# The weights of a one-core diffusion layer, laid out so that each partition's part of a buffer slot is one run in memory

## The chip, the cores and the metric

The kernel runs on one core of a Trainium2 chip. The metric is the device time of one execution in microseconds (us), lower is better. The core has a matrix engine (PE, with its weight loads shown apart as PEld), a vector engine (DVE), a scalar engine (ACT), GpSimd (POOL) and a sequencer for transfers (SP). SP issues every load of this kernel; 16 DMA engines carry them out in the order of issue. A transfer is carried as packets; a packet moves one run of bytes that is contiguous at both ends.

## The reference, cut to what matters

```python
mod = jax.nn.silu(c) @ w_ada[l] + b_ada[l]                 # w_ada 1024 x 6144: six vectors for scale, shift and gate
h = modulate(rms_norm(x, g_pre_mix[l]), sh1, sc1)          # x: 256 tokens x 1024
q, k, v, su, sv = split_projection(h @ w_in[l] + b_in[l])
...                                                        # windowed attention beside spatial gating (sgu_w)
mix = merge_heads(attn_o, sgu_o, ..., w_out[l], b_out[l])  # w_out 1024 x 1024
x_mid = x + gt1 * rms_norm(mix, g_post_mix[l])
h2 = modulate(rms_norm(x_mid, g_pre_ffn[l]), sh2, sc2)
# 32 experts, each token goes to its top 4 by h2 @ w_router + b_router; for an expert's tokens xb:
gu = xb @ w_gate_up[e] + b_gate_up[e]                      # w_gate_up[e]: 1024 x 2048
act = (up + 1) * gate * jax.nn.sigmoid(SWIGLU_ALPHA * gate)
y = act @ w_down[e] + b_down[e]                            # w_down[e]: 1024 x 1024
x_new = x_mid + gt2 * rms_norm(ffn, g_post_ffn[l])
```

All numbers are float32. The experts' weights are 32 x 12 MB, and all of them are read, whatever the routing.

## The kernel before

**Stages.** The first part (up to about 194 us) computes the mixing sub-layer and the routing. Its order is the text `PLAN`, a list of step names; a step is a Python generator (`step(...)`) whose pieces run as its name comes up. Then a loop goes over the 32 experts. For an expert, `gu_chunk` multiplies the expert's up to 64 tokens by four chunks of `w_gate_up` (64 matmuls into the PSUM banks `pg` and `pu`), `swiglu` and `to_ff` make the activations on DVE, ACT and PE, and `down` multiplies them by two chunks of `w_down` (32 matmuls into `py`). Experts come in pairs: `gather_pair` makes the pair's tokens (`gx`), `combine` adds the pair's results to the output (`cb`). An expert with more than 64 tokens takes the branches `more_gu` and `more_down` (bank `pm`); two of the 32 do with these inputs, and the branch is jumped over for the others.

**Slots.** Weights lie in ten slots of 128 partitions x 16 KB (2 MB each), made by `slot`; slot 6 is two halves of 8 KB per partition (`slot_halves`, tiles `we_a` and `we_b`). `order` gives the turn of the slots and `todo` the order of the loads: `load_chunk` for the chunks of an expert (four of `w_gate_up`, two of `w_down`), `load_gt2` for two pieces of `w_ada`, and `load_columns` at the end for `w_down` of the last two experts, by columns. `load_more(n)` issues the next n loads; SP waits in each until the slot's former content is used up. Loads for the experts begin during the first part (`ring` in `PLAN`).

**Where the bytes lie.** In memory the weights lie as in the reference, row by row. A slot of `w_gate_up` takes 256 rows of 8 KB: partition p gets rows p and 128 + p, two runs of 8 KB. A slot of `w_down` takes 512 rows of 4 KB: four runs of 4 KB a partition. `load_ada` takes 256 columns at a time out of rows of 24 KB (runs of 1 KB), and `load_columns` 512 or 256 columns (runs of 2 KB or 1 KB). In the halves of slot 6 the runs are as long as in a whole slot. All loads go through `load`, which is `SY.dma_start`; in profiles they have the line of the helper that records every operation (L114).

Of the kernel before, what the change touches and what calls it, by code (L numbers as in the profile page):

```python
# [20 lines left out]
P = 128  # L21
D = 1024
T = 256
KD = D // P
HEADS = 8
HD = 64
NE = 32
SL = 64
SM = 32
NSLOT = 10  # L30
# [52 lines left out]
def kernel(  # L83
# [5 lines left out]
    rows: bass.AP,  # L89
    cst: bass.AP,  # L90
    w_ada: bass.AP,
    w_in: bass.AP,
    w_out: bass.AP,
    sgu_w: bass.AP,
# [1 line left out]
    w_gate_up: bass.AP,  # L96
    b_gate_up: bass.AP,
    w_down: bass.AP,
    b_down: bass.AP,
    out: bass.AP,  # L100
):
# [28 lines left out]
    def slot(i, name, dt=F32):  # L130
        return ring.tile([P, 4096], dt, tag=f"s{i}", name=name)

    def slot_halves(i, name, dt=F32):

        if i == SPLIT:
            return [ring.tile([P, 2048], dt, tag=f"s{i}{h}", name=f"{name}_{h}") for h in "ab"]
        w = slot(i, name, dt)
        return [w[:, 0:2048], w[:, 2048:4096], w]
# [5 lines left out]
    def load(dst, src):  # L144
        SY.dma_start(out=dst, in_=src)
# [58 lines left out]
    ada = []  # L204
    win = [None] * KD

    def load_ada(i):
        a = slot(i % 2, f"ada{i}").rearrange("p (k c) -> p k c", k=KD)
        src = w_ada.rearrange("(k p) c -> p k c", p=P)
        load(a[:, :, 0:256], src[:, :, 256 * i:256 * i + 256])  # L210
        load(a[:, :, 256:512], src[:, :, D + 256 * i:D + 256 * i + 256])
        ada.append(a)

    def load_win(i):
        w = slot(2 + i % 2, f"win{i}")[:, 0:2 * 1792].rearrange("p (k c) -> p k c", k=2)
# [11 lines left out]
    hT, cT = s8[:, 0], s8[:, 1]  # L227
    kvs = slot(7, "kvs", FR).rearrange("p (k s c) -> p k s c", k=KD, s=2)
    load_ada(0)
    load_win(0)  # L230
    load_ada(1)


# [22 lines left out]
    wr = pre.tile([P, KD, NE], F32, name="wr")  # L256
    halves = [slice(0, 512), slice(512, 1024)]
# [9 lines left out]
    tiles = {}  # L267
# [215 lines left out]
    ada2 = {}  # L483

    def load_mod(i, j, a):
        a = a.rearrange("p (k c) -> p k c", k=4)
        load(a, w_ada[512 * j:512 * j + 512, D * i:D * i + D].rearrange("(k p) c -> p k c", p=P))
        return a

    def mod_half(pm, a, j):  # L490
        for b in range(4):
# [10 lines left out]
           adav[:, 8 * i:8 * i + 8].rearrange("p (n c) -> p n c", n=2), ADD)  # L502

    def load_rest(j, sl):
        a = slot(sl, f"adb{j}").rearrange("p (k c) -> p k c", k=2)
        load(a, w_ada[256 * j:256 * j + 256, 2048:4096].rearrange("(k p) c -> p k c", p=P))
        ada2[j] = a
        yield

    def load_scale2(j, sl):  # L510
        tiles["sc2", j] = load_mod(4, j, slot(sl, f"adc{j}"))
        yield

    def load_ws():
        wsraw = slot(0, "ws")[:, 0:1024].rearrange("p (h j) -> p h j", h=HEADS)
        load(wsraw, sgu_w.rearrange("h i j -> i h j"))
        tiles["ws"] = wsraw
        yield

    def load_wr():  # L520
        load(wr, w_router.rearrange("(k p) e -> p k e", p=P))
        yield

    def load_context():
# [8 lines left out]
    wo = [None, None]  # L533

    def load_wo(i, sl):
        w = slot(sl, f"wo{i}").rearrange("p (k c) -> p k c", k=4)
        load(w, w_out[512 * i:512 * i + 512, :].rearrange("(k p) c -> p k c", p=P))
        wo[i] = w
        yield


# [9 lines left out]
    order = [6, 9, 1, 3, 7, 4, 8, 0, 2, 5]  # L551
    cursor = [0]
    chunks = {}

    def load_weights(e, rows, srcs):

        halves = slot_halves(order[cursor[0] % NSLOT], f"we{e}_{cursor[0]}")
        cursor[0] += 1
        w = [h.rearrange("p (k c) -> p k c", k=rows // 2) for h in halves[0:2]]
        for c, src in srcs:  # L560
            src = src.rearrange("(k p) c -> p k c", p=P)
            if len(halves) > 2:
                load(halves[2].rearrange("p (k c) -> p k c", k=rows)[:, :, c], src)
            else:
                for i in range(2):
                    load(w[i][:, :, c], src[:, rows // 2 * i:rows // 2 * (i + 1), :])
        return w

    def load_chunk(e, j):

        if j < 4:
            return load_weights(e, 2, [(slice(0, 2048), w_gate_up[e, 256 * j:256 * j + 256, :])])
        return load_weights(e, 4, [(slice(0, D), w_down[e, 512 * (j - 4):512 * (j - 3), :])])

    def load_columns(e, n, step):

        return load_weights(e, 8, [(slice(c, c + step), w_down[e, :, 512 * n + c:512 * n + c + step])
                                   for c in range(0, 512, step)])

    gt2_parts = []  # L580

    def load_gt2(j):
        gt2_parts.append(load_mod(5, j, slot(order[cursor[0] % NSLOT], f"adg{j}")))
        cursor[0] += 1

    todo = [(load_chunk, (e, j)) for e in range(NE) for j in range(6 if e < NE - 2 else 4)]
    todo += [(load_columns, (e, n, 256 if e == NE - 1 else 512)) for n in range(2) for e in (NE - 2, NE - 1)]
    todo[18:18] = [(load_gt2, (j,)) for j in range(2)]
    loaded = [0]

# [497 lines left out]
    for i in R4:  # L1088
        step(f"mod{i}", modulation(i))
        step(f"adb{i}", load_rest(i, 1 + i))  # L1090
        if i > 1:
            step(f"ada{i}", load_ada_win(load_ada, i))
        if i > 0:
            step(f"win{i}", load_ada_win(load_win, i))
# [4 lines left out]
    step("bias", bias_in())  # L1099
    step("lctx", load_context())  # L1100
    step("lws", load_ws())
    step("lwr", load_wr())
    step("cnorm", context_norm())
    step("ring", load_ring())
    step("braw", load_braw())
    step("bparts", bias_parts())
    step("wo0", load_wo(0, 2))
    step("wo1", load_wo(1, 0))
    step("oproj", open_proj())
    step("oscore", open_scores())  # L1110
# [8 lines left out]
    for t in R2:  # L1119
        for q in R2:  # L1120
# [9 lines left out]
            for n in R2:  # L1130
                step(f"w{t}{q}{n}", w_out_half(t, q, n))
        step(f"adc{t}", load_scale2(t, (1, 3)[t]))
        step(f"krope{t}", key_rope(t))
        step(f"qrope{t}", query_rope(t))
# [105 lines left out]

    def wd(w, f, c0, n):

        if w[4][0].shape[1] == 4:
            return w[4 + c0 // 512][f // 4][:, f % 4, c0 % 512:c0 % 512 + n]
        return w[4 + f // 4][f % 4 // 2][:, f % 2, c0:c0 + n]

    def down(w, aT, ye):
        py = bank(2, "py")
        for f in range(8):
            c, q = f // 4, f % 4  # L1250
            for n in range(2):
                PE.matmul(py[64 * n:64 * n + 64, :], lhsT=aT[:, q, 64 * c:64 * c + 64], rhs=wd(w, f, 512 * n, 512),
                          start=f == 0, stop=f == 7)
        S.copy(ye[:, 0:512], py[0:64, :])
        V.tensor_copy(out=ye[:, 512:1024], in_=py[64:128, :])
# [159 lines left out]
    def rest(cm, aT):  # L1415

        more_aT[0] = aT
        first = cursor[0]
        with tc.If(cm > SL + SM):
            for e in range(NE):  # L1420
                cv = count(e)
                for b in range(SL if e < LATE else SL + SM, T, SM):
                    with tc.If(cv > b):
                        cursor[0] = first
                        w = [load_chunk(e, j) for j in range(4)]
                        more_gu(e, b, w, 0)
                        cursor[0] = first
                        w += [load_chunk(e, j) for j in (4, 5)]
                        more_down(w, 0)
        cursor[0] = first  # L1430
# [31 lines left out]
    for e in range(NE):  # L1462
        p, j = e // 2, e % 2
        last = e == NE - 1
        w, more, cv = chunks[e], {}, None
# [65 lines left out]
    for t in range(2):  # L1531
        v = cs[:, C_TRI + 8 + t:C_TRI + 9 + t]
# [11 lines left out]
def shape_constants():  # L1544
    t = np.arange(T)
    n_freq = HD // 4
    inv = (np.float32(10000.0) ** (-np.arange(n_freq, dtype=np.float32) / np.float32(n_freq))).astype(np.float32)
    ar = ((t // 64).astype(np.float32)[:, None] * inv).astype(np.float32)
    ac = ((t % 64).astype(np.float32)[:, None] * inv).astype(np.float32)
    cos = np.stack([np.cos(ar), np.cos(ar), np.cos(ac), np.cos(ac)], 1).reshape(T, 64)  # L1550
    sin = np.stack([-np.sin(ar), np.sin(ar), -np.sin(ac), np.sin(ac)], 1).reshape(T, 64)
    c = np.zeros((P, C_W), np.float32)
    c[:, C_ID:C_ID + P] = np.eye(P)
    c[:, C_COS:C_COS + P] = cos.reshape(2, P, 64).transpose(1, 0, 2).reshape(P, P)
    c[:, C_SIN:C_SIN + P] = sin.reshape(2, P, 64).transpose(1, 0, 2).reshape(P, P)
    c[:, C_IOTA:C_IOTA + SL] = np.arange(1, SL + 1)
    c[:, C_TRI:C_TRI + P] = np.triu(np.ones((P, P)), 1)
    c[:, C_E96:C_E96 + NE] = np.arange(P)[:, None] % NE == np.arange(NE)
    return c
# [26 lines left out]
```

## Time and profile before

| | |
|---|---|
| median of 3 runs | 1172.83 us (1172.65 to 1174.62) |
| profiled execution, its own time | 1177.28 us |
| its span, first to last instruction | 1175.5 us |
| PE busy | 1073.3 us, 91% of the span |
| DVE, ACT, POOL busy | 343.4, 149.8, 110.2 us |
| DMA | 446.21 MB, 90590 packets, mean 380 GB/s |
| mean granted TensorE clock | 0.961 of full speed |

The profile comes from one execution that took 4.45 us more than the median of the runs. Busy PE time is modelled from pipelined matmuls, so a high share does not mean that PE works at its peak. A DMA share of 1 means that all 16 DMA engines carry packets all the time.

### The profile page before, as it was taken

Reading aid. Unit: us, or ns where it says so; the run is one execution under the profiler, and the core shown is the slowest. Engines: PE = TensorE matmul, PEld = TensorE weight load, DVE = VectorE, ACT = ScalarE, POOL = GpSimd, SP = SyncE. Lnnn points to the kernel's source line nnn. Section 1 sums busy time; section 2 is a strip of 40 time slices with the busy share of each in tenths; the row PEclk is TensorE's granted clock in tenths of the full one; section 3 lists DMA queues with packets and bytes.
Section 4 is the critical chain, followed back from the end, with each engine's and each line's share of the span. In section 5 each row is a group of like instructions: output and inputs, shape, how many; then the busy total and the mean of one; then the engine's idle time right before and its main releaser. Section 6 shows DMA issues by size and latency. Waiting matters only on the chain. (4 is left out here: it accounts for less than half of the span.)

```text
span 1175.5 us, 14247 instructions
## 1 busy us (share of the span) xinstructions
PE 1073.3 (91%) x5653; PEld 525.3 (45%) x5653; DVE 343.4 (29%) x763; ACT 149.8 (13%) x308; POOL 110.2 (9%) x199
## 2 busy tenths in 40 slices
PE   6998979999999997999999998888989988999995
PEld 5865536343535443445353534343424353353534
DVE  4698543112122212212212121212121221322123
ACT  4653111111000000000000000000000000000011
POOL 2235252000000000000000000000000000000001
PEclk9998988899999998899999999999999997899997
DMA  9976866999999999999999999999999999899981
GB/s 335 388 292 248 339 222 238 391 415 417 416 417 415 416 416 417 416 411 415 416 416 417 416 416 416 417 416 415 417 416 412 413 418 417 345 417 416 418 290 38
DMA packets 90590, 446.21 MB, mean 380 GB/s; under 512 B 5105, under 2 KB 18529, under 8 KB 56577
## 3 DMA queue, kind: packets, MB, share of 16 engines
q1 hardware_dynamic: 90466, 444.47, 94.1%
q8 instruction: 88, 1.44, 0.5%
q14 instruction: 36, 0.29, 0.1%
HBM read 443.41 MB, written 1.05 MB: 378 GB/s over the span
## 5 line engine op out<-in xcount | busy, mean ns | idle before, releaser
L114 PE MATMUL pg<-we,xT 128*64 128x512 f32 x872 | 233.7, 605 | 32.9 <-DMA we<-in_w_gate_up_dram 28.4
L114 PE MATMUL pu<-we,xT 128*64 128x512 f32 x872 | 231.1, 598 | 0.0
L114 PE MATMUL py<-we,g 128*64 128x512 f32 x848 | 195.0, 606 | 4.2 <-ACTq L1341 3.8
L114 PEld LDWEIGHTS pg<-we,xT 128*64 128x64 f32 x872 | 67.0, 138 | 162.4 <-issue 119.3
L114 PEld LDWEIGHTS py<-we,g 128*64 128x64 f32 x848 | 90.1, 140 | 95.4 <-issue 78.2
L114 DVE TENSOR_SCALAR g<-pg 128x512 f32<-128x512 f32 x31 | 21.4, 691 | 380.4 <-PE pg L114 367.4
L114 PEld LDWEIGHTS pu<-we,xT 128*64 128x64 f32 x872 | 72.3, 138 | 117.9 <-issue 117.9
L114 DVE COPY ye<-py 64x512 f32<-64x512 f32 (+2 forms) x36 | 22.8, 635 | 276.6 <-ACTq L1341 210.3
L114 POOL TENSOR_TENSOR xT<-xT,sh 128x512 f32<-128x512 f32 x30 | 31.2, 1039 | 770.6 <-DVE xT L114 762.2
L114 ACT ACTIVATE sg<-g 128x512 f32<-128x512 f32 (+1 forms) x34 | 21.4, 630 | 463.5 <-DVE g L114 463.5
L114 PEld LDWEIGHTS gx<-oh,xs 128*128 128x128 f32 x544 | 66.3, 202 | 18.0 <-PE pg L114 10.5
L114 PE MATMUL gx<-oh,xs 128*128 128x128 f32 (+1 forms) x544 | 69.5, 287 | 4.7 <-DVE oh L114 4.7
L114 PE MATMUL cb<-ye,ohT 128*128 128x512 f32 (+1 forms) x132 | 57.9, 581 | 0.5 <-DVE ye L114 0.5
L114 ACT COPY ye<-py 64x512 f32<-64x512 f32 (+2 forms) x36 | 19.1, 530 | 253.9 <-PE py L114 253.9
L114 DVE TENSOR_TENSOR yacc<-cb,yacc 128x512 f32<-128x512 f32 (+1 forms) x74 | 46.1, 671 | 12.3 <-PE cb L114 12.3
L114 PE MATMUL wo<-wo,proj 128*128 128x512 f32 x64 | 31.5, 632 | 9.4 <-DVE proj L114 9.4
L114 PEld LDWEIGHTS cb<-ye,ohT 128*128 128x128 f32 x132 | 23.7, 190 | 23.0 <-issue 15.2
L114 DVE TENSOR_TENSOR xT<-gx,a 128x512 f32<-128x512 f32 x30 | 20.7, 688 | 14.3 <-PE gx L114 14.3
L114 ACT COPY g<-aT 128x512 f32<-128x512 f32 x30 | 17.6, 585 | 51.0 <-PE aT L114 47.7
L114 DVE TENSOR_TENSOR u<-u,sg 128x512 f32<-128x512 f32 x32 | 22.2, 692 | 3.8 <-ACT sg L114 0.5
L114 DVE TENSOR_SCALAR u<-pu 128x512 f32<-128x512 f32 x31 | 21.4, 691 | 5.1 <-PE pu L114 5.1
L114 DVE SCALAR_TENSOR_TENSOR u<-u,g 128x512 f32<-128x512 f32 x32 | 22.1, 692 | 1.1
(389 smaller groups left out, 1013.9 us busy)
## 6 DMA issues: line engine op xcount, KB each, us to landing
we<-in_w_gate_up_dram SPq DMA_DIRECT2D x116, 2048.0 KB, 25.0
we<-in_w_down_dram SPq DMA_DIRECT2D x54, 2048.0 KB, 29.7
we_a<-in_w_gate_up_dram SPq DMA_DIRECT2D x12, 1024.0 KB, 23.7
we_b<-in_w_gate_up_dram SPq DMA_DIRECT2D x12, 1024.0 KB, 18.7
ada<-in_w_ada_dram SPq DMA_DIRECT2D x8, 1024.0 KB, 13.0
adb<-in_w_ada_dram SPq DMA_DIRECT2D x4, 2048.0 KB, 8.8
we_a<-in_w_down_dram SPq DMA_DIRECT2D x8, 1024.0 KB, 25.6
we_b<-in_w_down_dram SPq DMA_DIRECT2D x8, 1024.0 KB, 26.5
```

Source lines behind the costliest of these rows:

```text
L114: inst = call(*args, **kwargs)
```

## The change

The host lays out every weight except `w_in` so that what a partition gets in one slot (or half of a slot) is one run in memory: the helper `runs` regroups rows (k p) to (p k). `w_ada` becomes three tensors (`w_ada` for `load_ada`, `w_adb` for `load_rest`, `w_adc` for `load_mod`), and the columns of the last two experts' `w_down` become `w_last`. The loads then name `[128, 4096]` or `[128, 2048]` blocks that are contiguous in memory. The places of all values in the slots stay, except for the last expert's columns, which now lie as two halves of 256 columns; `wd` finds them there. The host's work is not part of the measured time.

```diff
     def load_ada(i):
-        a = slot(i % 2, f"ada{i}").rearrange("p (k c) -> p k c", k=KD)
-        src = w_ada.rearrange("(k p) c -> p k c", p=P)
-        load(a[:, :, 0:256], src[:, :, 256 * i:256 * i + 256])
-        load(a[:, :, 256:512], src[:, :, D + 256 * i:D + 256 * i + 256])
-        ada.append(a)
+        a = slot(i % 2, f"ada{i}")
+        for b in range(2):
+            load(a[:, 2048 * b:2048 * b + 2048], w_ada[i, :, 2048 * b:2048 * b + 2048])
+        ada.append(a.rearrange("p (k c) -> p k c", k=KD))
...
     def load_mod(i, j, a):
-        a = a.rearrange("p (k c) -> p k c", k=4)
-        load(a, w_ada[512 * j:512 * j + 512, D * i:D * i + D].rearrange("(k p) c -> p k c", p=P))
-        return a
+        load(a, w_adc[i, j])
+        return a.rearrange("p (k c) -> p k c", k=4)
...
-    def load_weights(e, rows, srcs):
+    def load_weights(e, rows, src, split=False):
 
         halves = slot_halves(order[cursor[0] % NSLOT], f"we{e}_{cursor[0]}")
         cursor[0] += 1
-        w = [h.rearrange("p (k c) -> p k c", k=rows // 2) for h in halves[0:2]]
-        for c, src in srcs:
-            src = src.rearrange("(k p) c -> p k c", p=P)
-            if len(halves) > 2:
-                load(halves[2].rearrange("p (k c) -> p k c", k=rows)[:, :, c], src)
-            else:
-                for i in range(2):
-                    load(w[i][:, :, c], src[:, rows // 2 * i:rows // 2 * (i + 1), :])
-        return w
+        if len(halves) > 2 and not split:
+            load(halves[2], src)
+        else:
+            for i in range(2):
+                load(halves[i], src[:, 2048 * i:2048 * i + 2048])
+        return [h.rearrange("p (k c) -> p k c", k=rows // 2) for h in halves[0:2]]
 
     def load_chunk(e, j):
 
-        if j < 4:
-            return load_weights(e, 2, [(slice(0, 2048), w_gate_up[e, 256 * j:256 * j + 256, :])])
-        return load_weights(e, 4, [(slice(0, D), w_down[e, 512 * (j - 4):512 * (j - 3), :])])
...
+        return load_weights(e, 2, w_gate_up[e, j]) if j < 4 else load_weights(e, 4, w_down[e, j - 4])
...
+    def load_columns(e, n):
+
+        return load_weights(e, 8, w_last[0, n]) if e < NE - 1 else load_weights(e, 16, w_last[1, n], True)
...
+    runs = lambda v, k: a(v.reshape(v.shape[:-2] + (-1, k, P, v.shape[-1])).swapaxes(-3, -2)).reshape(
+        v.shape[:-2] + (-1, P, k * v.shape[-1]))
...
+        "w_gate_up": runs(a(w_gate_up)[0], 2), "b_gate_up": a(b_gate_up)[0], "w_down": runs(wd, 4),
```

`load_rest`, `load_wo`, `load_ws` and `load_wr` change in the same way as `load_mod`. No instruction changes its place on any engine; what changes is the shape that SP's loads name. Here are SP's rows in the expert loop (names: tile of the slot `<-` tensor in memory, then partitions x runs x elements of a run; `we_20_a` and `we_20_b` are the halves of slot 6, and the branch rows are the jumps over `more_gu` and `more_down`), before:

```order
L114 DMA adg_2064<-in_w_ada_dram 128x4x1024
L114 DMA we_20_a<-in_w_gate_up_dram 128x2048
L114 DMA we_20_b<-in_w_gate_up_dram 128x2048
L1341 UNCONDITIONAL_BRANCH
L114 DMA we_21_2204<-in_w_gate_up_dram 128x2x2048
L114 DMA we_22_2297<-in_w_gate_up_dram 128x2x2048
L114 DMA we_23_2307<-in_w_gate_up_dram 128x2x2048
L114 DMA we_24_2317<-in_w_down_dram 128x4x1024
```

and the same rows of SP in the changed kernel:

```order
L117 DMA adg_2064<-in_w_adc_dram 128x4096
L117 DMA we_20_a<-in_w_gate_up_dram 128x2048
L117 DMA we_20_b<-in_w_gate_up_dram 128x2048
L1338 UNCONDITIONAL_BRANCH
L117 DMA we_21_2204<-in_w_gate_up_dram 128x4096
L117 DMA we_22_2297<-in_w_gate_up_dram 128x4096
L117 DMA we_23_2307<-in_w_gate_up_dram 128x4096
L117 DMA we_24_2317<-in_w_down_dram 128x4096
```

The rows stand in the same order; two or four runs a partition became one of 4096 elements (16 KB), and a half of slot 6 with `w_gate_up` names what it named before. At the start of the program SP's rows, before:

```order
L114 DMA rows<-in_rows_dram 1x3880
L114 DMA ada_81<-in_w_ada_dram 128x8x256 x2
L114 DMA win_84<-in_w_in_dram 128x1792 x2
L114 DMA ada_87<-in_w_ada_dram 128x8x256 x2
L114 DMA ada_267<-in_w_ada_dram 128x8x256 x2
```

and in the changed kernel:

```order
L117 DMA rows<-in_rows_dram 1x3880
L117 DMA ada_81<-in_w_ada_dram 128x2048 x2
L117 DMA win_84<-in_w_in_dram 128x1792 x2
L117 DMA ada_87<-in_w_ada_dram 128x2048 x2
L117 DMA ada_267<-in_w_ada_dram 128x2048 x2
```

Here eight runs of 1 KB a partition became one of 8 KB, and `win`, the loads of `w_in`, stayed as they were.

## Rows read from the trace of the kernel before

**Rows 1.** Stages: us, busy time by engine, granted clock, DMA share, GB/s.
```profile
0.00:195.00 195.00, 168.24 (x1141) 116.00 (x1143) 121.14 (x307) 71.47 (x158) 71.93 (x159) 0.94 0.80 296
195.00:300.00 105.00, 101.34 (x486) 41.45 (x483) 21.71 (x56) 13.27 (x25) 2.69 (x4) 0.97 0.99 394
300.00:690.00 390.00, 375.55 (x1863) 174.54 (x1861) 91.80 (x175) 28.78 (x53) 15.16 (x15) 0.98 1.02 416
690.00:960.00 270.00, 237.60 (x1129) 102.56 (x1129) 56.57 (x111) 17.63 (x31) 10.39 (x10) 0.99 1.02 415
960.00:1030.00 70.00, 62.35 (x318) 25.59 (x316) 15.95 (x33) 4.83 (x10) 0.62 (x1) 0.80 0.96 387
1030.00:1142.00 112.00, 110.40 (x549) 51.40 (x547) 26.04 (x46) 7.97 (x14) 4.15 (x4) 1.00 1.00 398
1142.00:1175.50 33.50, 17.80 (x184) 13.80 (x180) 10.20 (x38) 5.82 (x19) 5.29 (x6) 0.81 0.10 34
```

**Rows 2.** PE's waits, 195 to 690 us: what for, us, times, longest.
```profile
PE aT L114 <- DVE g L114: 3.8, 1, 3.8
...
PE py L114 <- DMA we<-in_w_gate_up_dram: 0.4, 1, 0.4
```

**Rows 3.** PE's waits, 690 to 960 us, all of them.
```profile
PE pg L114 <- DMA we<-in_w_gate_up_dram: 28.4, 25, 2.9
PE py L114 <- ACTq L1341: 1.6, 4, 0.4
PE pg L114 <- PEq L1341: 1.3, 6, 0.3
```

**Rows 4.** PE's waits, 960 us to the end: the longest of eight, none on a DMA.
```profile
PE py L114 <- PEq L1419: 5.4, 1, 5.4
```

**Rows 5.** PE in order of time, 715 to 742 us: start, us, work [idle before].
```profile
722.91 1.08 PE L114 MATMUL pg<-we,xT 128*64 128x512 f32 x4 [0.39 <-DMA we<-in_w_gate_up_dram]
...
727.96 1.08 PE L114 MATMUL pg<-we,xT 128*64 128x512 f32 x4 [1.39 <-DMA we<-in_w_gate_up_dram]
...
732.85 1.08 PE L114 MATMUL pg<-we,xT 128*64 128x512 f32 x4 [1.24 <-DMA we<-in_w_gate_up_dram]
```

**Rows 6.** Loads issued from 195.5 to 918.8 us: count, KB each, us to landing.
```profile
we<-in_w_gate_up_dram SPq DMA_DIRECT2D x87, 2048.0 KB, 25.9
we<-in_w_down_dram SPq DMA_DIRECT2D x42, 2048.0 KB, 30.6
we_a<-in_w_gate_up_dram SPq DMA_DIRECT2D x9, 1024.0 KB, 24.8
...
we_a<-in_w_down_dram SPq DMA_DIRECT2D x6, 1024.0 KB, 27.6
...
adg<-in_w_ada_dram SPq DMA_DIRECT2D x2, 2048.0 KB, 17.5
```

**Rows 7.** Packets in 1050 to 1063, 1038 to 1045 and 1135 to 1137.3 us.
```profile
DMA packets 715, 5.47 MB, mean 421 GB/s; under 512 B 48, under 2 KB 48, under 8 KB 48
...
DMA packets 916, 3.70 MB, mean 411 GB/s; under 512 B 27, under 2 KB 27, under 8 KB 902
...
DMA packets 777, 0.81 MB, mean 350 GB/s; under 512 B 14, under 2 KB 753, under 8 KB 777
```

**Rows 8.** Packets and one load in 2 to 7 us.
```profile
DMA packets 620, 1.54 MB, mean 309 GB/s; under 512 B 57, under 2 KB 235, under 8 KB 619
...
rows<-in_rows_dram SPq DMA_DIRECT2D x1, 15.2 KB
```

**Rows 9.** The page's queue of instruction loads: packets, MB, share of 16 engines.
```profile
q8 instruction: 88, 1.44, 0.5%
```

**Rows 10.** PE's waits in 10 to 100 us: the longest, and the one on a DMA.
```profile
PE xT L114 <- DVE xn_a L114: 3.1, 1, 3.1
...
PE mod L114 <- DMA ada<-in_w_ada_dram: 0.2, 1, 0.2
```

More of the change, by code (lines that the diff above doesn't have):

```diff
@@ L91 @@
     w_ada: bass.AP,
+    w_adb: bass.AP,
+    w_adc: bass.AP,
     w_in: bass.AP,
@@ L98 @@
     w_down: bass.AP,
+    w_last: bass.AP,
     b_down: bass.AP,
@@ L504, in load_rest @@
     def load_rest(j, sl):
-        a = slot(sl, f"adb{j}").rearrange("p (k c) -> p k c", k=2)
-        load(a, w_ada[256 * j:256 * j + 256, 2048:4096].rearrange("(k p) c -> p k c", p=P))
-        ada2[j] = a
+        a = slot(sl, f"adb{j}")
+        load(a, w_adb[j])
+        ada2[j] = a.rearrange("p (k c) -> p k c", k=2)
         yield
     def load_scale2(j, sl):
-        tiles["sc2", j] = load_mod(4, j, slot(sl, f"adc{j}"))
+        tiles["sc2", j] = load_mod(0, j, slot(sl, f"adc{j}"))
         yield
     def load_ws():
-        wsraw = slot(0, "ws")[:, 0:1024].rearrange("p (h j) -> p h j", h=HEADS)
-        load(wsraw, sgu_w.rearrange("h i j -> i h j"))
-        tiles["ws"] = wsraw
+        wsraw = slot(0, "ws")[:, 0:1024]
+        load(wsraw, sgu_w)
+        tiles["ws"] = wsraw.rearrange("p (h j) -> p h j", h=HEADS)
         yield
     def load_wr():
-        load(wr, w_router.rearrange("(k p) e -> p k e", p=P))
+        load(wr.rearrange("p k e -> p (k e)"), w_router)
         yield
@@ L535, in load_wo @@
     def load_wo(i, sl):
-        w = slot(sl, f"wo{i}").rearrange("p (k c) -> p k c", k=4)
-        load(w, w_out[512 * i:512 * i + 512, :].rearrange("(k p) c -> p k c", p=P))
-        wo[i] = w
+        w = slot(sl, f"wo{i}")
+        load(w, w_out[i])
+        wo[i] = w.rearrange("p (k c) -> p k c", k=4)
         yield
@@ L553 @@
     chunks = {}
-    def load_weights(e, rows, srcs):
+    def load_weights(e, rows, src, split=False):
         halves = slot_halves(order[cursor[0] % NSLOT], f"we{e}_{cursor[0]}")
         cursor[0] += 1
-        w = [h.rearrange("p (k c) -> p k c", k=rows // 2) for h in halves[0:2]]
-        for c, src in srcs:
-            src = src.rearrange("(k p) c -> p k c", p=P)
-            if len(halves) > 2:
-                load(halves[2].rearrange("p (k c) -> p k c", k=rows)[:, :, c], src)
-            else:
-                for i in range(2):
-                    load(w[i][:, :, c], src[:, rows // 2 * i:rows // 2 * (i + 1), :])
-        return w
-    def load_chunk(e, j):
-        if j < 4:
-            return load_weights(e, 2, [(slice(0, 2048), w_gate_up[e, 256 * j:256 * j + 256, :])])
-        return load_weights(e, 4, [(slice(0, D), w_down[e, 512 * (j - 4):512 * (j - 3), :])])
-    def load_columns(e, n, step):
-        return load_weights(e, 8, [(slice(c, c + step), w_down[e, :, 512 * n + c:512 * n + c + step])
-                                   for c in range(0, 512, step)])
+        if len(halves) > 2 and not split:
[4 more added lines that the diff above has]
+        return [h.rearrange("p (k c) -> p k c", k=rows // 2) for h in halves[0:2]]
+    def load_chunk(e, j):
+        return load_weights(e, 2, w_gate_up[e, j]) if j < 4 else load_weights(e, 4, w_down[e, j - 4])
+    def load_columns(e, n):
+        return load_weights(e, 8, w_last[0, n]) if e < NE - 1 else load_weights(e, 16, w_last[1, n], True)
     gt2_parts = []
     def load_gt2(j):
-        gt2_parts.append(load_mod(5, j, slot(order[cursor[0] % NSLOT], f"adg{j}")))
+        gt2_parts.append(load_mod(1, j, slot(order[cursor[0] % NSLOT], f"adg{j}")))
         cursor[0] += 1
     todo = [(load_chunk, (e, j)) for e in range(NE) for j in range(6 if e < NE - 2 else 4)]
-    todo += [(load_columns, (e, n, 256 if e == NE - 1 else 512)) for n in range(2) for e in (NE - 2, NE - 1)]
+    todo += [(load_columns, (e, n)) for n in range(2) for e in (NE - 2, NE - 1)]
     todo[18:18] = [(load_gt2, (j,)) for j in range(2)]
@@ L1241, in wd @@
     def wd(w, f, c0, n):
+        if w[4][0].shape[1] == 8:
+            return w[4 + c0 // 512][c0 % 512 // 256][:, f, c0 % 256:c0 % 256 + n]
         if w[4][0].shape[1] == 4:
@@ L1569 @@
     wo = a(w_out)[0]
+    wo = np.concatenate([perm(wo[0:512]), wo[512:]], 0)
+    ada = a(w_ada)[0]
+    wd = a(w_down)[0]
+    runs = lambda v, k: a(v.reshape(v.shape[:-2] + (-1, k, P, v.shape[-1])).swapaxes(-3, -2)).reshape(
+        v.shape[:-2] + (-1, P, k * v.shape[-1]))
     vecs = np.concatenate([r(b_ada), r(g_pre_mix), r(g_pre_ffn), r(g_post_mix), r(g_post_ffn),
@@ L1574 @@
         "x": a(x)[0], "cx": a(ctx)[0], "vecs": vecs, "rows": rows,
-        "cst": shape_constants(), "w_ada": a(w_ada)[0], "w_in": a(w_in)[0], "w_out": np.concatenate([perm(wo[0:512]), wo[512:]], 0),
-        "sgu_w": a(sgu_w)[0], "w_router": a(w_router)[0], "w_gate_up": a(w_gate_up)[0],
-        "b_gate_up": a(b_gate_up)[0], "w_down": a(w_down)[0], "b_down": a(b_down)[0],
+        "cst": shape_constants(),
+        "w_ada": runs(ada[:, 0:2 * D].reshape(D, 2, 4, 256).transpose(2, 0, 1, 3).reshape(4, D, 512), KD)[:, 0],
+        "w_adb": runs(ada[:, 2 * D:4 * D], 2),
+        "w_adc": runs(ada[:, 4 * D:6 * D].reshape(D, 2, D).swapaxes(0, 1), 4),
+        "w_in": a(w_in)[0], "w_out": runs(wo, 4),
+        "sgu_w": a(a(sgu_w)[0].swapaxes(0, 1)).reshape(P, 1024), "w_router": runs(a(w_router)[0], KD)[0],
+        "w_gate_up": runs(a(w_gate_up)[0], 2), "b_gate_up": a(b_gate_up)[0], "w_down": runs(wd, 4),
+        "w_last": np.stack([runs(wd[NE - 2].reshape(D, 2, 512).swapaxes(0, 1), KD)[:, 0],
+                            runs(wd[NE - 1].reshape(D, 2, 2, 256).transpose(1, 2, 0, 3), KD)[:, :, 0].swapaxes(1, 2)
+                            .reshape(2, P, 4096)]), "b_down": a(b_down)[0],
     }
+    ins = {k: a(v) for k, v in ins.items()}
     nc = bacc.Bacc("TRN2", target_bir_lowering=False, num_devices=1)
```

## Prediction

> **What bounds the kernel now.** I read first the stages, to see where DMA and where PE is full; then PE's waits stage by stage; then how fast packets of each size move; then which loads stand in the stage that counts. The chain of work that ended last is of no use here: it reaches back only through the end of the program.
>
> In the stages [rows 1] the reader is to look at the DMA share and at PE together. Up to 195 us the share is 0.80. From 195 to 960 us it is 0.99 to 1.02: all 16 engines carry packets all the time. From 195 to 690 us PE is busy too and waits 0.4 us for a load in total [rows 2]. From 690 to 960 us it waits 28.4 us, 25 times, always for a chunk of `w_gate_up`, and for nearly nothing else [rows 3]; the granted clock there is 0.99, so the clock is not the cause. In PE's order of time one sees the tempo: the first matmuls on three successive chunks start at 722.91, 727.96 and 732.85 us [rows 5], 5.05 and 4.89 us apart, which is about what a slot takes to arrive (below). After 960 us, where a full expert takes the extra branch at a granted clock of 0.80, PE falls behind, the slots fill up, and PE waits for no load any more [rows 4]: from there to the end it is PE's own work that counts.
>
> So PE consumes faster than the loads come, lives on the ten full slots until about 690 us, and then goes at the pace of the loads. One queue feeds it: a load issued in 195.5 to 918.8 us lands some 26 to 31 us after its issue [rows 6], behind about five others. A load that takes less time therefore brings every later one forward, also in the stretch where PE does not wait yet, and the sum of what is saved from 195 us on comes out of the 28.4 us.
>
> **What a packet costs.** The page does not show a weight packet of 16 KB, so I work it out from three stretches in which nearly all bytes move in one size [rows 7]. With runs of 8 KB: 421 GB/s, 26.3 GB/s for one engine, 8192 B in 311 ns. With 4 KB: 411 GB/s, 159.5 ns a packet, 319.0 for 8 KB, so the second packet costs 7.6 ns. With 1 KB: 350 GB/s, 46.8 ns a packet; eight take 374.5 ns, 63 more than one of 8 KB, 9.0 ns for each of seven. I take 8 ns of fixed cost per packet. A packet of 16 KB should then take 2 x 311 - 8 = 615 ns, 426 GB/s, and a slot of 2 MB 4.92 us in place of 4.98 (8 KB runs) or 5.10 (4 KB runs).
>
> The Trainium skill, "DMA: Bandwidth & Descriptors", section Specifications, names 512 B as the smallest transfer that moves at line rate. By that rule alone nothing here would gain and the time would stay at 1172.8 us. The trace does not agree: 350 GB/s with 1 KB beside 421 with 8 KB.
>
> **The change part by part.** PE, DVE, ACT and POOL keep every instruction and its place, and SP its order; only the runs get longer.
>
> 1. Loads of the expert loop up to the last one for which PE waits, those issued from 195.5 to 918.8 us [rows 6]. A slot has 128 partitions, 8 for each of 16 engines.
> - 87 whole slots of `w_gate_up`: 16 packets an engine become 8; 8 x 8 ns = 0.064 us each, 5.6 us.
> - 42 whole slots of `w_down`: 32 become 8; 24 x 8 = 0.192 us each, 8.1 us.
> - 2 pieces of `w_ada` (`adg`): also 32 to 8, 0.4 us.
> - 6 pairs of halves with `w_down`: 32 become 16 over the pair; 0.128 us each, 0.8 us.
> - 9 pairs of halves with `w_gate_up`: 8 KB before and after, nothing.
> Sum 14.9 us. It fits into the 28.4 us, so 13.5 us of waiting on loads should stay and the DMA remains what is late next in that stage. Bounds: with 7.6 and 9.0 ns instead of 8, 14.2 and 16.8 us. Should nothing be gained beyond 8 KB, the `w_gate_up` slots give nothing and `w_down` 0.128 us a slot: 5.4 + 0.3 + 0.8 = 6.4 us. Should a 16 KB packet have no fixed cost left, another 8 ns on 8 packets of 131 slots, 8.4 us, come on top: 23.3 us. The waits cap it at 28.4 us.
>
> 2. Loads before 195 us. The eight `w_ada` loads of 1 MB save most a piece (64 packets an engine become 8, 0.45 us each, 3.6 us in all); `adb`, `adc`, `wo`, `ws` and `wr` get shorter too. Between 10 and 100 us PE waits 0.2 us for a load, on the first of `w_ada` [rows 10]; its work, in the order of `PLAN`, hides the rest, and without that cover the 3.6 us would count. Only the first two stand ahead of PE's first use, 0.9 us at most. Between 0 and 0.9 I take 0.4 us, nearer the row's wait.
>
> 3. Loads issued after 918.8 us, the columns of the last two experts among them (1 KB and 2 KB runs become 8 and 16 KB). They get shorter by the most, and PE waits for none of them [rows 4]: nothing. What hides them is PE's lag after 960 us; DMA has a share of 0.10 in the last 33.5 us [rows 1].
>
> 4. The issue of a load waits for its slot, not for SP, and its waits stay: nothing.
>
> Sum: 14.9 + 0.4 = 15.3 us. The profiled execution took 1177.28 us (span 1175.5) and would take 1162.0. The median of the runs is 4.45 us shorter than it; no row says where, and I take the same saving: 1172.83 - 15.3 = **1157.5 us**.
>
> **The rivals.**
>
> - *Longer than 8 KB gains nothing*, because the engines cut such runs or because the cost per packet is no cost per packet. Time 1172.8 - 6.4 - 0.4 = 1166.0. For it: no weight run over 8 KB was ever moved. Against it: of the packets in 2 to 7 us exactly one (620 less 619) is 8 KB or more, and the load of 15.2 KB in one partition is issued there [rows 8], so a run of that length went as one packet. 0.10.
> - *More is gained than packets*, since a partition's reads no longer jump in memory between its runs. 1172.8 - 23.7 = 1149.1, at most 1172.8 - 28.4 = 1144.4, where PE would be the bound everywhere. For it: 1 KB runs, which jump most, cost 9.0 ns a packet, a little more than the 7.6 of the others. 0.10. The same page of the Trainium skill, section "Where 436 GB/s comes from", puts the ceiling at 435 GB/s; the estimate from it is 4.82 us a slot and 27 us saved, close to the cap, and no row comes near that rate.
> - *A packet of 16 KB is slow.* The only packets of that size on the page are the 88 of instruction loads, which took 0.5% of 16 x 1175.5 us, 1.07 us each [rows 9], far over 615 ns. The place is every whole slot from 195 us on. The gain of 14.9 us is 14 ns on each of 131 x 8 packets, so from 629 ns on the change loses; at 660 ns it is 31 x 8 x 131 = 32 us slower (1205), and at 1.07 us a slot takes 8.6 us and the time is some 460 us more. Against it: instruction packets share each engine with a weight packet of 311 ns, which alone lengthens them, and nothing in [rows 7] bends upward with size. 0.06.
> - *It does not show.* An instruction packet that takes turns with weight packets would now wait 0.3 us longer for its turn; 51 exposed ones of the 88 undo 15.3 us. PE's waits on a sequencer are 2.9 us in all from 690 to 960 us [rows 3], 5.4 at a jump after 960 [rows 4]; so few are exposed. 1172.8, 0.06, the case of a line rate reached at short runs included.
>
> **How the numbers follow.** The forecast, 1152 to 1163 us, gets 0.68; the others 0.10, 0.10, 0.06 and 0.06. Two times of this kernel differ visibly from about 0.2% (2.3 us) on. Faster by more than that: 0.68 + 0.10 + 0.10 = 0.88; within it 0.06; slower 0.06. The range, 1147 to 1167 us, takes in the forecast, the cut at 8 KB (1166.0) and the nearer part of the larger gain (1149.1); it leaves out the cap and the last two rivals.
>
> **What the profile of the changed kernel would show.** In a stretch of whole slots alone some 426 GB/s in place of 421 and 411, and first matmuls on successive waited-for chunks 4.9 us apart. In all some 36,000 packets in place of 90,590. PE's waits for `w_gate_up` in the late stage near 13.5 us in place of 28.4, beginning later than 690 us. The first 195 us nearly unchanged, and no load waited for at the end. I would be wrong if the rate of whole slots stays at 421 (cut, or memory-bound) or goes below it, if PE's waits shrink less than the loads (another wait in their place), or if a later start of the extra branch costs PE more at a low granted clock.

## The result, and the profile after

The changed kernel takes 1158.59 us (median of 4 runs, 1156.41 to 1159.75), the kernel before 1172.74 us (4 runs). The ratio is 0.9871, with a 95% interval of 0.9853 to 0.9890: 15.1 us less, between 12.9 and 17.2 (the two medians alone lie 14.15 us apart). The forecast was 1157.5 us, 15.3 us less. The profiled execution took 1159.75 us, with a span of 1157.9 us; its counterpart before took 1177.28 and 1175.5.

The stages of the changed kernel (columns as in [rows 1]: length, busy time by engine, granted clock, DMA share, GB/s):

```profile
0.00:195.00 195.00, 169.14 (x1147) 116.46 (x1149) 122.34 (x313) 72.92 (x161) 72.03 (x159) 0.94 0.76 296
195.00:300.00 105.00, 101.34 (x504) 43.34 (x501) 23.03 (x53) 12.30 (x21) 2.82 (x5) 0.98 1.00 413
300.00:690.00 390.00, 375.57 (x1852) 173.54 (x1852) 91.46 (x178) 29.19 (x53) 15.06 (x15) 0.98 1.00 420
690.00:960.00 270.00, 244.72 (x1176) 112.17 (x1175) 57.05 (x113) 18.00 (x32) 11.02 (x11) 0.98 1.01 426
```

In the stage where PE waits for loads the rate went from 415 to 426 GB/s, the figure forecast for packets of 16 KB, and the DMA share is still 1.01: the loads are still the bound. From 300 to 690 us only 420 stand, which is taken up below. The page's count of packets:

```profile
DMA packets 36574, 446.21 MB, mean 385 GB/s; under 512 B 4081, under 2 KB 4321, under 8 KB 6657
```

The same bytes move in 36574 packets, not 90590. PE's waits from 690 to 960 us, to lay beside [rows 3]:

```profile
PE pg L117 <- DMA we<-in_w_gate_up_dram: 18.2, 13, 2.9
PE gx L117 <- DVE oh L117: 2.5, 2, 2.3
PE py L117 <- ACTq L1338: 1.9, 4, 0.5
```

13 waits of 18.2 us for a load stand where 25 of 28.4 us stood. The first of them comes at 751.92 us, where it came at 697.79 us. (The second row is the start of the second extra branch, which now falls into this window.) PE in order of time in that stage, as in [rows 5]:

```profile
887.39 1.08 PE L117 MATMUL pg<-we,xT 128*64 128x512 f32 x4 [0.52 <-DMA we<-in_w_gate_up_dram]
...
889.13 1.06 PE L117 MATMUL pg<-we,xT 128*64 128x512 f32 x4
889.99 1.06 PE L117 MATMUL pu<-we,xT 128*64 128x512 f32 x4
892.18 1.08 PE L117 MATMUL pg<-we,xT 128*64 128x512 f32 x4 [1.14 <-DMA we<-in_w_gate_up_dram]
...
902.01 1.08 PE L117 MATMUL pg<-we,xT 128*64 128x512 f32 x4 [1.15 <-DMA we<-in_w_gate_up_dram]
```

Four chunks begin between 887.39 and 902.01 us, 4.87 us apart on average. Four groups of matmuls do a chunk, 0.86 us apart when nothing is waited for, so PE needs 3.4 us of the 4.87. The rows also show why the waits shrank less than the time: a group is drawn 1.06 us long, so 0.2 us of each wait lies under it and is not counted.

Where the 17.6 us between the two spans come from shows at three marks, here in the trace of before (start us, us, work):

```profile
193.88 1.94 PE L114 MATMUL gu<-we_a,yacc 128*64 128x512 f32 x8
...
964.75 7.22 PE L114 MATMUL gx<-oh,xs 128*128 128x32 f32 x32 [2.31 <-DVE oh L114]
...
1027.31 1.08 PE L114 MATMUL pg<-we,xT 128*64 128x512 f32 x4 [0.16 <-PEq L1341]
```

and in the trace of the changed kernel:

```profile
192.62 1.94 PE L117 MATMUL gu<-we_a,yacc 128*64 128x512 f32 x8
...
949.51 0.38 PE L117 MATMUL gx<-oh,xs 128*128 128x32 f32 x2 [2.31 <-DVE oh L117]
...
1009.95 1.08 PE L117 MATMUL pg<-we,xT 128*64 128x512 f32 x4 [0.16 <-PEq L1338]
```

The first mark is the first expert matmul, the second the start of the second extra branch, the third the next expert behind it. The changed kernel is earlier by 1.3, 15.2 and 17.4 us. So 1.3 us came before the expert loop, 14.0 us in the stretch that the forecast priced at 14.9, 2.1 us in the extra branch and 0.2 us after it. Each trace is one execution; the one of before took 4.5 us more than the median above, the other 1.2 us, so the 17.6 us are some 3.4 us more than the medians differ by.

### The profile page after: what moved, and what is told of

Its sections match the earlier page's. It is cut to its first block, busy times and chain, and to the rows that moved or that the text cites. A ratio compares the mean times of both kernels' runs of the same rounds, so it can differ in the third digit from the quotient of the medians.

```text
span 1157.9 us, 14247 instructions
## 1 busy us (share of the span) xinstructions
PE 1066.3 (92%) x5653; PEld 526.6 (45%) x5653; DVE 343.6 (30%) x763; ACT 150.1 (13%) x308; POOL 110.4 (10%) x199
## 2 busy tenths in 40 slices
DMA packets 36574, 446.21 MB, mean 385 GB/s; under 512 B 4081, under 2 KB 4321, under 8 KB 6657
## 5 line engine op out<-in xcount | busy, mean ns | idle before, releaser
L117 PE MATMUL pg<-we,xT 128*64 128x512 f32 x872 | 233.1, 603 | 22.7 <-DMA we<-in_w_gate_up_dram 18.2
L117 DVE TENSOR_SCALAR g<-pg 128x512 f32<-128x512 f32 x31 | 21.4, 692 | 366.5 <-PE pg L117 353.5
L117 ACT ACTIVATE sg<-g 128x512 f32<-128x512 f32 (+1 forms) x34 | 21.4, 630 | 449.0 <-DVE g L117 449.0
L117 PEld LDWEIGHTS cb<-ye,ohT 128*128 128x128 f32 x132 | 23.7, 190 | 23.0 <-issue 15.2
L117 ACT COPY g<-aT 128x512 f32<-128x512 f32 x30 | 17.6, 586 | 51.4 <-PE aT L117 48.1
L117 DVE TENSOR_SCALAR u<-pu 128x512 f32<-128x512 f32 x31 | 21.4, 692 | 5.5 <-PE pu L117 5.5
## 6 DMA issues: line engine op xcount, KB each, us to landing
win<-in_w_in_dram SPq DMA_DIRECT2D x8, 896.0 KB, 11.5
```

Source lines behind the costliest of these rows:

```text
L117: inst = call(*args, **kwargs)
```

## The experiments

Two theories: **the packet** (each packet costs some 8 ns beside its bytes, in a stretch that the loads bound) and **the place** (what counts is where and how contiguously the bytes lie in memory). A third, **the cut**, says that nothing is gained beyond 8 KB. Times are medians; each ratio is to runs of the kernel before on the same chip.

| run | time us | ratio to before, 95% interval |
|---|---|---|
| `w_gate_up` alone | 1167.63 | 0.9949 (0.9932 to 0.9966) |
| `w_down` alone | 1163.87 | 0.9925 (0.9909 to 0.9941) |
| all but the experts | 1172.99 | 0.9993 (0.9979 to 1.0007) |
| `w_gate_up` in 4 KB runs | 1177.48 | 1.0037 (1.0023 to 1.0051) |
| runs 2 MB apart | 1173.37 | 1.0005 (0.9988 to 1.0023) |
| runs 2 MB + 16 KB apart | 1159.92 | 0.9890 (0.9865 to 0.9914) |
| before, no extra branch | 1154.08 | 0.9838 (0.9807 to 0.9869) |
| changed, no extra branch | 1132.69 | 0.9670 (0.9638 to 0.9703) |

**One part alone.** The kernel before with new loads for `w_gate_up` (`load_block` issues a slot, or two halves, from `[128, 4096]`):

```diff
-            return load_weights(e, 2, [(slice(0, 2048), w_gate_up[e, 256 * j:256 * j + 256, :])])
+            return [h.rearrange("p (k c) -> p k c", k=1) for h in load_block(w_gate_up[e, j])[0:2]]
...
+        "w_gate_up": runs(a(w_gate_up)[0], 2),
```

> The kernel before, with only the chunks of w_gate_up laid out as one run of 16 KB a partition. Theory (a fixed cost per packet, in a stretch that the loads bound): 87 whole slots at 8 packets an engine less, 0.064 to 0.08 us each by the two traces, so 5.6 to 7.0 us faster than before, about 1166. Rival (runs beyond 8 KB gain nothing): no change, 1172.7.

The ratio is worth 6.0 us (4.0 to 8.0). The same for `w_down` of the first 30 experts:

```diff
-        return load_weights(e, 4, [(slice(0, D), w_down[e, 512 * (j - 4):512 * (j - 3), :])])
+        return [h.rearrange("p (k c) -> p k c", k=2) for h in load_block(w_dr[e, j - 4])[0:2]]
...
+        "w_dr": runs(a(w_down)[0], 4),
```

> The kernel before, with only the chunks of w_down (of the first 30 experts) laid out as one run of 16 KB a partition. Theory: 42 whole slots at 24 packets an engine less (0.19 to 0.22 us each) and 6 pairs of halves (0.13 to 0.16 us), so 8.9 to 10.2 us faster, about 1163. Rival (nothing beyond 8 KB): 16 packets less count, 0.128 us for 42 and 6 slots, 6.1 us, 1166.6.

8.8 us (6.9 to 10.7). And the changed kernel with the experts' loads as before:

```diff
-        return load_weights(e, 2, w_gate_up[e, j]) if j < 4 else load_weights(e, 4, w_down[e, j - 4])
+        if j < 4:
+            return load_weights(e, 2, [(slice(0, 2048), w_gate_up[e, 256 * j:256 * j + 256, :])])
+        return load_weights(e, 4, [(slice(0, D), w_down[e, 512 * (j - 4):512 * (j - 3), :])])
```

> The changed kernel with the experts' weights and their loads as before: only w_ada, w_out, sgu_w and w_router keep the new layout. By the prediction's terms 0.4 us from the start and 0.4 us from the two pieces of w_ada in the expert loop, 0.8 us; by the start of the expert loop in the trace of the changed kernel, 1.2 us earlier, up to 1.6 us: 1171 to 1172. Rival (the 3.6 us saved on the early loads count in full): 1168.7.

0.8 us (2.5 faster to 0.8 slower): no change that can be told, and the 3.6 us that the early loads save do not count. The parts add up, within their intervals: 6.0 + 8.8 + 0.8 = 15.6 beside 15.1. The first run rules out the cut; the second alone would do so only just, since its interval begins at 6.9 and the cut gives 6.1. Spread over the packets that the forecast counted for an engine, the 6.0 us are 8.6 ns for each of 87 x 8 (5.7 to 11.5 by the interval), and the 8.8 us are 8.0 ns for each of 42 x 24 + 6 x 16 (6.3 to 9.7).

**Shorter packets in the same block.** The changed kernel, a slot of `w_gate_up` still 2 MB in one block, but in four runs of 4 KB a partition:

```diff
+        if e is not None and rows == 2:
...
+                        load(halves[2].rearrange("p (q c) -> p q c", q=4), src.rearrange("q p c -> p q c"))
...
+        "w_gate_up": a(runs(a(w_gate_up)[0], 2).reshape(NE, 4, P, 4, 1024).transpose(0, 1, 3, 2, 4)),
```

> The changed kernel, but a slot of w_gate_up comes as four runs of 4 KB a partition; the slot is still one block of 2 MB in memory. Theory (cost per packet): 87 whole slots at 24 packets an engine more (0.19 to 0.22 us) and 9 pairs of halves at 16 more (0.13 to 0.16), 18 to 20.5 us slower than the changed kernel, 1177 to 1179, slower than before. Rival (it is the contiguous block in memory that counts, not the length of a packet): 1158.6.

1.0037 less 0.9871 is 19.5 us slower than the changed kernel, and slower than before: 8.7 ns for each of 87 x 24 + 9 x 16 packets. The contiguous block alone is worth nothing. The rate at which the loads go shows it in one row each, 700 to 940 us of before, then of the changed kernel, then of `w_down` alone (columns as in [rows 1]):

```profile
700.00:940.00 240.00, 211.04 (x992) 89.66 (x988) 49.94 (x96) 15.83 (x28) 8.31 (x8) 0.99 1.02 415
```

```profile
700.00:940.00 240.00, 217.65 (x1047) 96.51 (x1044) 54.03 (x102) 17.06 (x30) 9.74 (x10) 0.99 1.01 426
```

```profile
700.00:940.00 240.00, 216.46 (x1020) 92.99 (x1017) 50.76 (x98) 16.00 (x29) 8.33 (x8) 0.99 1.01 422
```

415, 426 and 422 GB/s at a full DMA share; `w_gate_up` in 4 KB runs gives this, 700 to 950 us:

```profile
700.00:950.00 250.00, 215.82 (x1018) 90.82 (x1016) 49.95 (x96) 15.85 (x28) 8.32 (x8) 1.00 1.02 414
```

**The same packets in other places.** The changed kernel with neighbouring partitions' runs of `w_gate_up` 2 MB apart, and then 2 MB and 16 KB apart (padding 4096 elements instead of 0):

```diff
-        return load_weights(e, 2, w_gate_up[e, j]) if j < 4 else load_weights(e, 4, w_down[e, j - 4])
+        return load_weights(e, 2, w_gate_up[:, 4096 * (4 * e + j):4096 * (4 * e + j) + 4096]) if j < 4 else load_weights(e, 4, w_down[e, j - 4])
...
+        "w_gate_up": np.pad(runs(a(w_gate_up)[0], 2).reshape(4 * NE, P, 4096).swapaxes(0, 1).reshape(P, 4 * NE * 4096), ((0, 0), (0, 0))),
```

> The changed kernel, but the 16 KB runs of neighbouring partitions of w_gate_up lie 2 MB apart in memory, not one behind the other. Theory (only the packet's length counts): as the changed kernel, 1158.6. Rival (where the runs lie in memory counts; the Trainium skill, DMA: Bandwidth & Descriptors, section Latency and other measured facts, has a slower rate at row pitches of large powers of two, 164 GB/s at 2 MiB beside 214): loads slower than before, and the time well over 1173.

> As the run with runs 2 MB apart, with 16 KB more between them. Both theories: about the changed kernel's 1158.6; if the run without the extra 16 KB is slow and this one is not, it is the power of two that counts, and not that the runs lie apart.

The first loses the whole gain (1.0005), the second keeps it (0.9890, whose interval holds the changed kernel's 0.9871). So packets of 16 KB alone are not enough: at a pitch of exactly 2 MB they come more slowly, although no other thing in the kernel differs. Stretches without an extra branch, with the pitch of 2 MB:

```profile
300.00:440.00 140.00, 135.41 (x646) 62.29 (x646) 31.53 (x58) 10.68 (x19) 6.08 (x6) 1.00 1.00 412
700.00:950.00 250.00, 221.07 (x1030) 93.12 (x1032) 49.94 (x96) 15.85 (x28) 8.32 (x8) 0.99 1.01 419
```

and with the 16 KB more:

```profile
300.00:440.00 140.00, 137.13 (x667) 65.10 (x667) 33.69 (x62) 10.68 (x19) 6.24 (x6) 1.00 1.01 426
700.00:950.00 250.00, 226.77 (x1090) 100.81 (x1086) 54.12 (x103) 17.65 (x31) 10.40 (x10) 1.00 1.01 425
```

412 and 419 GB/s beside 426 and 425. The direction is that of the Trainium skill ("DMA: Bandwidth & Descriptors", Latency and other measured facts), and so is the cure by padding, 16 KB here and 4 KiB there; the size is not: a loss of 1 to 3% here, where the page has about a quarter, for copies between tensors in memory. "Well over 1173" was wrong. In the trace not every packet is slower: of the 16 KB packets from 700 to 940 us, the median is 611 ns in the run with 2 MB and 613 ns with 16 KB more, but 6% of them take more than 650 ns in the first and 0.4% in the second. Why this pitch is slow no run here tells.

**Without the extra branches.** Both kernels with the branches never taken; they leave out the work for tokens beyond 64 of an expert:

```diff
     def rows_left(cv, step):
-        with tc.If(cv > SL):
+        with tc.If(cv > T):
             step()
```

> The kernel before, leaving out the work for tokens beyond 64 of an expert (the branches more_gu and more_down are never taken). Theory (the loads bound the expert loop; PE is the bound late only because of the second extra branch): PE waits for loads to the end, the last load lands about when it did, and the time falls little, to about 1160. Rival (PE bound): the two branches' 35 to 38 us each come off, about 1100.

> The changed kernel, leaving out the work for tokens beyond 64 of an expert. Theory: now all loads to the end count, 109 whole slots of w_gate_up (7 to 8.7 us), 51 of w_down (9.8 to 11.2), the halves and pieces (1.5) and the last columns (2.6), and 1.2 us from the start: 22 to 25 us less than the same kernel before without the branches. Rival (what was saved is what can be saved): 14 to 15 us less.

The kernel before falls by 19 us, not by the 70 that a PE-bound kernel would give back, and PE now waits for loads also after 960 us. It falls to 1154, 6 us below the expected 1160: the loads had moved at 387 GB/s from 960 to 1030 us, about the second branch [rows 1], and now move at 418 GB/s from 960 to 1100 us, which is an estimated 5 us over these 70 us. PE's waits for loads after 960 us, before without branches and then changed without branches:

```profile
PE pg L114 <- DMA we<-in_w_gate_up_dram: 19.9, 16, 2.9
```

```profile
PE pg L117 <- DMA we<-in_w_gate_up_dram: 12.6, 13, 1.4
```

In [rows 4] there was none. With the branches gone the change is worth 0.9670 / 0.9838 = 0.983, 19.7 us by the ratios and 21.4 by the medians, a little under the 22 to 25 expected and more than the 15.1 with branches. Four runs each, spread over 4.8 and 5.4 us, leave this uncertain by some 4 us, so the rival's 14 to 15 us are out, but not by much. The branches, then, cap what the layout gives. Both were left out at once, so these two runs do not tell the late one, behind which nobody waits for loads, from the first, which costs loading time of its own (next section).

## Why the prediction was right

*What bounds the kernel.* Shown: a change in the shape of the loads alone moves the time, up (packets of 4 KB) and down, by about what the rates of loading give, and without the branches PE waits for loads to the end. The waits begin later than before, as forecast.

*The cost of a packet.* 8 ns were taken, from stretches at 411, 421 and 350 GB/s; the times of three runs gave 8.0, 8.6 and 8.7 ns, each uncertain by 1 to 3 ns. The rate for 16 KB was forecast as 426 GB/s and is 426. But these prices come from whole times, which also hold what the branches give or take; by the rates alone a packet costs some 9 to 10 ns, as the next part works out.

*Part 1, the expert loop.* 14.9 forecast, 14.0 in the profiles. The number is right partly by luck, because two errors nearly cancel. The first: the loads of [rows 6] are 146 slots, 306 MB; at 426 in place of 415 or 416 GB/s they take 17 to 19 us less, more than the 14.9. That is 9 to 10 ns for each of the 1848 packets that an engine no longer carries. The prices taken from stretches of one size, 4.98 and 5.10 us a slot, make 418 GB/s for the mix of before, which went at 415 or 416; what slows the mix is open. The second: at the first extra branch the faster loads now fill all slots while PE is held up, and DMA runs dry. The same 20 us before and then after (columns as in [rows 1]):

```profile
480.00:500.00 20.00, 18.94 (x130) 10.48 (x128) 7.66 (x12) 1.94 (x4) 2.08 (x2) 0.84 1.02 415
```

```profile
480.00:500.00 20.00, 18.94 (x136) 11.40 (x138) 6.95 (x11) 1.87 (x4) 2.08 (x2) 0.91 0.84 341
```

341 GB/s for 20 us instead of 426 is 4.0 us of loading not done, which is most of why 420 stood from 300 to 690 us. What SP waited for most from 430 to 520 us, before and then after (us in total, times, longest):

```profile
SPq L114 <- PE pu L114: 23.2, 6, 8.6
```

```profile
SPq L117 <- PE pu L117: 42.9, 8, 21.2
```

SP waits up to 21.2 us for PE to be done with a slot, and without the branches the changed kernel moves 427 GB/s in the same 20 us. The forecast looked for such a lag only at the second branch.

*Part 2, the start.* 0.4 us forecast. The run with all but the experts, which also holds 0.4 us of Part 1, gave 0.8 us, as much as both together, but with an interval about zero. The 1.3 us by which the loop began earlier in the profile say little: in the two profiles whose code is the same up to there and differs from the changed kernel only in where `w_gate_up` lies, it began at 191.10 and 195.16 us. What moves it is not settled.

*Part 3, the end.* Nothing, as forecast (0.2 us); PE waits for no load after 960 us in the changed kernel either.

*Part 4, the issue.* The price, nothing, was right, the reason wrong: see the last section.

*The waits.* 13.5 us should have stayed, 18.2 did: the waits shrank by less than the loads, which the forecast had named as a sign of being wrong. Of the 4.7 us, 2.4 are the counting (12 waits fewer hide 0.2 us each) and 0.9 are Part 1 (14.0 in place of 14.9). The other 1.4 us stay open.

*Not foreseen.* The second extra branch took 2.1 us less, with a granted clock of 0.83 instead of 0.79 in its stretch (949 to 1010 us beside 964 to 1028). The other profiles say that it is more than the accident of one pair: from the first mark of the branch to the next expert it took 62.6 us before, 62.7 in all but the experts and 62.6 with runs 2 MB apart; 60.4 in the changed kernel, 60.5 with `w_down` alone and 60.5 with runs 2 MB + 16 KB apart; 61.4 with `w_gate_up` alone and 61.2 in 4 KB runs. So in these profiles 1 to 2 us of the gains come from the branch and not from the loads; why, no run tells.

*The rivals.* The cut is out by the run with `w_gate_up` alone; slow packets of 16 KB are out by the rate; a line rate reached at short runs is out by the runs of 4 KB. The larger gain from memory order is not seen: all three packet prices come out alike, and a packet of 8 KB takes 313 ns (median in 690 to 940 us) both before, where a partition's two runs lie 1 MB apart, and in the changed kernel, where its half slot is one run. That the gain might not show is out by the time itself; the 88 packets of instruction loads took 1.06 us each on average, 1.07 before.

## What to carry to other kernels

First show that loads are the bound where PE waits (DMA share at 1, waits on loads, chunk starts a slot's load time apart), then price a layout by packets: here 8 to 10 ns for each packet an engine no longer carries, for runs of 4 to 16 KB. Sum only over loads that stand ahead of the last wait, and look at every place where the slots can fill up, since there a faster queue stands still. Mind where the runs lie as well: the same runs 2 MB apart lost the whole gain, which one block and 16 KB of padding both kept.

## What the runs showed of the hardware that had not been expected

Before the change SP was held inside the load instructions themselves. The same loads of SP in 690 to 940 us, in the kernel before and then in the changed one (duration in ns: least, median, most; first and last start):

```profile
L114 SPq DMA_DIRECT2D we<-in_w_gate_up_dram x31: 411/2379/15360, 700.7 to 932.9; - x31
L114 SPq DMA_DIRECT2D we<-in_w_down_dram x14: 422/7466/11942, 706.8 to 923.3; - x14
```

```profile
L117 SPq DMA_DIRECT2D we<-in_w_gate_up_dram x29: 327/328/328, 702.9 to 926.5; - x29
L117 SPq DMA_DIRECT2D we<-in_w_down_dram x16: 327/328/328, 693.1 to 936.3; - x16
```

Issuing a load took up to 15.4 us with runs of 8 and 4 KB, and 0.33 us with 16 KB. It is not the shape of the load itself alone: in the run with `w_down` alone, the loads in 16 KB runs took up to 8.2 us too, among loads in 8 KB runs. What holds SP there is open. SP's longest waits show what holds it now:

```profile
SPq L117 <- DMA we<-in_w_gate_up_dram: 136.6, 30, 6.0
SPq L117 <- DMA we<-in_w_down_dram: 67.5, 15, 4.5
```

It waits for the landing of an earlier load, where before its longest wait in the same stretch was on PE's `pu` (107.3 us). With the DMA share at 1.01 and 1.02 both ways, neither costs time here.
